# Second block of a two-block network on one core: router and first gather taken on the raw residual sum, expert weights queued one by one, dense weight units, expert tail in halves

## The chip, the cores and the metric

The kernel runs on one core of a Trainium2 chip, as one program. The metric is the device time of one execution in microseconds (us). The engines are TensorE (PE; PEld is its weight load), VectorE (DVE), ScalarE (ACT), GpSimd (POOL) and SyncE (SP), which only issues DMAs here.

## The reference

256 tokens of width 1024 go through two layers of a first block and one layer of a second block, all in float32. The change lies at the end of the second block:

```python
x = x + g_m * hybrid_mixer(h, ...)            # ends in  merged @ w_out
h = rms_norm_2(x, norm_ffn) * (1.0 + sc_f) + sh_f
x = x + g_f * moe_ffn(h, w_router, b_router, w1, b1, w2, b2)

# moe_ffn: 32 experts, each token takes the best 4
logits = h @ w_router + b_router
top_v, top_e = lax.top_k(logits, 4);  weights = softmax(top_v)
hcat = h[tok] @ w1[e] + b1[e]                 # w1[e]: 1024 x 2048
x_glu = minimum(hcat[:, ::2], 7);  x_lin = clip(hcat[:, 1::2], -7, 7)
y = (x_glu * sigmoid(1.702 * x_glu) * (x_lin + 1)) @ w2[e] + b2[e]   # w2[e]: 1024 x 1024
```

The weights of 32 experts are 384 MB in units of 1 MB, and every one is read once.

## The kernel before

Activations stay in SBUF as two tiles of 128 tokens (t = 0, 1). Dense products (`gemm`, `products`, L205 to L207) split every weight granule of 128 x 1024 floats in a high and a low part (`load_split`, `split_from`: ACT at L143, DVE or POOL at L147) and add three products. Granules are loaded by SP (L219) into four buffers `raw`; the parts have seven buffers each.

The second block's mixer ends with `merge`: for each of six pairs (branch, half of the columns) a gate of four granules and, one pair later, a branch product of two. `merge` calls `then` once, in the second round: `prepare` queues the vector `gf`, the router's weights `wr` and bias `br`, the experts' first biases `b1` (by way of two of the four `raw` buffers), and the first four expert units back to back (`unit`, L1482). The compiler's planner orders each engine's stream from costs and due times; only what is pinned (`pin`, `pe`) keeps the program's order. The new buffers lie where the sliding-window attention (swa) had its scratch.

Then comes the last projection `w_out_2` (eight granules), one granule for both token tiles and the other seven tile by tile, each closed by `done`: scale and add the residual (L1262, L1263), `rms_mod` (sums of squares at L861, a reciprocal root by Newton steps at L124 to L138, the modulation at L872 and L873 with the full rows `A` and `sh`, transposes at L233 with copies at L878). `route` computes the logits (L1310), the best four (L1312 to L1320), the places of the tokens (L1322 to L1326) and the counts (L1329); `moe_gather` builds a one-hot matrix (L1357) and gathers the tokens of two experts by matmuls (L1369, copied out at L1372).

The expert stage `moe` takes two experts at a time, 24 units a pair: `moe_up` (L1417) with eight pairs of units, the activation (L1425 to L1430), transposes (`moe_aT`, L1439), `moe_down` (L1456) with four pairs of units, scaling (L1461) and `combine` (L1526, L1527), which for the last pair also writes the output (L1529). The units go round a ring of 18 buffers (`mtile`): four early ones, five more on the right side, nine where the granules of the dense products had been (`low`), the last one (`mods`, tile `AS`) where `A` and `sh` had been. A unit is issued when its buffer is free. Row p * 8 + j of a weight goes to partition p, so a unit takes 8 KB from each partition's stretch of 64 KB (w1) or 32 KB (w2). For the last pair the second half of w2 comes as four units split by columns (L1487, pieces of 2 KB).

Of the kernel before, what the change touches and what calls it, by code (L numbers as in the profile page):

```python
# [71 lines left out]
class Kernel:  # L72
    def __init__(self, tc, a, out, dbg=None):
        self.tc, self.nc, self.a, self.out, self.dbg = tc, tc.nc, a, out, dbg
        self.n = 0
        self.nraw, self.nhl, self.next, self.xp = 4, 7, 4, None
        self.npj, self.ngt, self.glag = 4, 4, 1
        self.dtail = 8
        self.xg = 4
        self.sp, self.late = None, False  # L80
        self.pre, self.npre = [], 4
        self.start = False
# [31 lines left out]

    def small(self, n, tag="sm", dt=F32):
# [4 lines left out]
    def rsqrt(self, v, eps, n, scale=1.0):  # L120
# [6 lines left out]
        y = self.small(n, "ry")  # L127
# [81 lines left out]
    def load_split(self, nk, w, c0, width, xn=0, onpool=()):  # L209
# [5 lines left out]
        for i in range(ng):  # L215
# [3 lines left out]
            nc.sync.dma_start(raw.rearrange("p (k n) -> p k n", n=width), self.wsrc(w, i * kpg, m, c0, width))  # L219
# [452 lines left out]
    def merge(self, mp, lhs, w_in, g0, wb, yTs, order, nk, then=None):  # L672
# [178 lines left out]
    def rms_mod(self, t, h, A, sh, split=True):  # L851

# [9 lines left out]
        self.normed = nc.vector.tensor_tensor(ss[:, 2:3], ss[:, 0:1], ss[:, 1:2], op=OP.add)  # L862
        r = self.rsqrt(ss[:, 2:3], 1e-6, 1, 1.0 / D)
        xT = self.new_xT(t)
        def part(v, c):

            return v[:, c * 512:c * 512 + 512] if split else v.rearrange("t (p k) -> t k p", k=KD)[:, 4 * c:4 * c + 4]

        for c in range(2):
            s = slice(c * 512, c * 512 + 512)  # L870
            hv = h[:, s] if split else h[:, s].rearrange("t (k p) -> t k p", k=4)
            nc.vector.scalar_tensor_tensor(hv, part(x, c), r[:, 0:1], part(A, c), op0=OP.mult, op1=OP.mult)  # L872
            nc.vector.tensor_tensor(hv, hv, part(sh, c), op=OP.add)  # L873
            if split:
                self.to_T(h, t, xT[0], xT[1], 4 * c, 4)
            else:
                pt = self.trans4([h[:, k * P:k * P + P] for k in range(4 * c, 4 * c + 4)])
                nc.scalar.activation(xT[0].bitcast(F32)[:, 4 * c:4 * c + 4, :],  # L878
                                     pt.rearrange("p (k q) -> p k q", q=P), AF.Copy)
# [311 lines left out]
    def hybrid_in(self, ctx, gp, first):  # L1191
# [3 lines left out]
        with tc.tile_pool(name="mix2", bufs=1, reuse_waits="tile") as mp:  # L1195
            gm = self.st(gp, [P, D], "gm")
            self.mod_row(gm, 2)
            A, sh = self.mod_pair(self.mods, 3, a["norm_ffn_2"][0])
# [39 lines left out]
            def prepare():  # L1238
                bp = self.bp = ctx.enter_context(tc.tile_pool(name="blk2", bufs=1, side="right", reuse_waits="tile"))
                self.gf = bp.tile([P, D], F32, name="gf")  # L1240
                self.mod_row(self.gf, 5)
                self.route_prep(bp)
                self.sel = self.selector(0)
                units(self.npre)
                self.mi = 0
                for src in self.sources(0)[:self.npre]:
                    self.pre.append(self.unit(src))

            mg = self.merge(mp, lhs, w, 3328, a["w_branch_2"][0], yTs, (1, 0, 2), 4, prepare)
# [3 lines left out]
        units(self.na - self.npre)  # L1253
        hp = ctx.enter_context(tc.tile_pool(name="h2", bufs=1, side="right", reuse_waits="tile"))
        self.h2 = [hp.tile([P, D], F32, name=f"h{t}") for t in range(2)]
        with tc.tile_pool(name="y5", bufs=1, reuse_waits="tile") as fp:
            def done(t, banks):
                x = self.x[t]
                for h in range(2):
                    s = slice(h * 512, h * 512 + 512)  # L1260
                    y = self.st(fp, [P, 512], "y5", bufs=2)
                    nc.vector.scalar_tensor_tensor(y, banks[h], 0.5, gm[:, s], op0=OP.mult, op1=OP.mult)  # L1262
                    nc.vector.tensor_tensor(x[:, s], x[:, s], y, op=OP.add)  # L1263
                self.rms_mod(t, self.h2[t], A, sh, False)

            self.late = True
            self.gemm(self.lhs_x(mT), KD, a["w_out_2"][0], 0, D, done, tail=7)


    def route_prep(self, mp):  # L1270
        nc, a = self.nc, self.a
        wr = self.st(mp, [P, KD, NE], "wr")
        nc.gpsimd.dma_start(wr, a["w_router_2"][0].rearrange("(p k) n -> p k n", k=KD))
        br = self.st(mp, [P, NE], "br")
        nc.gpsimd.dma_start(br, arow(a["b_router_2"][0], NE))

        src = a["b1_2"][0].rearrange("e (j n) -> (e j) n", j=4)
        self.b1 = []
        for i in range(2):
            raw = self.st(self.wp, [P, 1024], "raw", bufs=self.nraw)[:, :512]  # L1280
            hl = self.st(mp, [P, 512], f"b1{i}", F32R)
            for h in range(2):
                nc.gpsimd.dma_start(raw[64 * h:64 * h + 64], src[64 * i:64 * i + 64])
            self.pin(nc.scalar.activation(hl, raw, AF.Copy))
# [3 lines left out]
        self.pin(nc.vector.tensor_tensor(self.pick, self.ident[:, :64], self.ident[:, 64:], op=OP.add))  # L1288
        tri = self.st(mp, [P, P], "tri")
        nc.vector.memset(tri, 1.0)  # L1290
# [3 lines left out]
        nc.vector.memset(one, 1.0)  # L1294
        self.rc = br, wr, tri, one

    def route(self, mp):

        nc, a = self.nc, self.a
        br, wr, tri, one = self.rc  # L1300
        self.W = self.st(mp, [P, 2, NE], "W")
        self.pos = self.st(mp, [P, 2, NE], "pos")
        mask = self.st(mp, [P, 2, NE], "mask")
        off = self.st(mp, [P, 2, NE], "off")
        cnt = self.st(mp, [P, NE], "cnt")
        for t in range(2):
            xT = self.xT[t][0].bitcast(F32)
            pl = self.ps("sc")[:, :NE]
            for k in range(KD):
                self.logits = nc.tensor.matmul(pl, xT[:, k, :], wr[:, k, :], start=k == 0, stop=k == KD - 1)  # L1310
            lg = self.st(mp, [P, NE], f"lg{t}")
            nc.vector.tensor_tensor(lg, pl, br, op=OP.add)  # L1312
            m8 = self.small(8, "m8")
            nc.vector.max(m8, lg)
            nm = self.small(1, "nm")
            nc.vector.tensor_scalar(nm, m8[:, 0:1], -1.0, None, op0=OP.mult)
            nc.vector.memset(m8[:, 4:8], 3.0e38)
            rep = self.st(mp, [P, NE], "rep")
            nc.vector.match_replace(rep, m8, lg, -3.0e38)
            nc.vector.tensor_tensor(mask[:, t], rep, lg, op=OP.not_equal)  # L1320
            pc = self.ps("sc")
            nc.tensor.matmul(pc[:, :NE], tri, mask[:, t], start=True, stop=t == 0)  # L1322
            if t:
                nc.tensor.matmul(pc[:, :NE], one, mask[:, 0], start=False, stop=True)
            nc.vector.tensor_scalar(off[:, t], mask[:, t], -BIG, BIG, op0=OP.mult, op1=OP.add)
            nc.vector.tensor_tensor(self.pos[:, t], off[:, t], pc[:, :NE], op=OP.add)  # L1326
            if t:
                for u in range(2):
                    nc.tensor.matmul(pc[:, NE:2 * NE], one, mask[:, u], start=u == 0, stop=u == 1)  # L1329
                nc.vector.tensor_copy(cnt, pc[:, NE:2 * NE])  # L1330
            ex = self.st(mp, [P, NE], f"ex{t}")
            nc.scalar.activation(ex, lg, AF.Exp, bias=nm)
# [3 lines left out]
            nc.vector.tensor_scalar(self.W[:, t], ex, sm, None, op0=OP.mult)  # L1336

# [5 lines left out]
        on = self.st(mp, [P, NE], "on")  # L1343
        nc.vector.memset(on, 1.0)
# [5 lines left out]
        self.Wh = self.st(mp, [P, 2, NE], "Wh")  # L1350
        nc.vector.tensor_scalar(self.Wh, self.W, 0.5, None, op0=OP.mult)

    def one_hot(self, mp, tag, pos):

        S = self.st(mp, [P, 2, 2, CAP], tag)
        for t in range(2):
            self.nc.vector.tensor_tensor(S[:, t], self.slot[:, None, :].to_broadcast([P, 2, CAP]),  # L1357
                                         pos[:, t, :, None].to_broadcast([P, 2, CAP]), op=OP.is_equal)
        return S

    def moe_gather(self, mp, pos):

        nc = self.nc
        S = self.one_hot(mp, "S", pos).rearrange("p t e s -> p t (e s)")
        xe = self.st(mp, [P, KD, P], "xe")
        pg = [self.ps("sc") for _ in range(2)]
        for t in range(2):
            for c in range(KD):
                self.pe(nc.tensor.matmul(pg[c // 4][:, c % 4 * P:c % 4 * P + P], self.h2[t][:, c * P:c * P + P], S[:, t],  # L1369
                                         start=t == 0 and c % 4 == 0, stop=t == 1 and c % 4 == 3))  # L1370
        for i in range(2):
# [391 lines left out]
```

## Time and profile before

| | us |
|---|---|
| median of 3 runs | 2553.19 (2549.77 to 2553.88) |
| the profiled execution | 2552.11 |
| its span, first to last instruction | 2550.5 |
| PE busy | 2385.5 (94%) |
| DVE, ACT, POOL busy | 1279.3, 817.6, 227.1 |
| mean granted clock of PE | 0.977 |
| moved by DMA | 707.49 MB |

Times in the rows count from the start of the span. Matmuls are pipelined, so a row's mean duration is more than the distance from one to the next. An arrow in brackets names what ended an engine's idle time.

### The profile page before, as it was taken

The page shows a single profiled execution, that of the slowest core. Times are in us where ns is not written, and L with a number is a line of the kernel's source. Part 1 is how long each engine was busy: PE and PEld are TensorE (multiplying, and loading weights), DVE is VectorE, ACT ScalarE, POOL GpSimd, SP SyncE. Part 2 cuts the span into 40 slices and gives each one's busy share as a digit, 9 for nine tenths or more (in the row PEclk, how much of TensorE's full clock was granted, in tenths as well). Part 3 has the DMA queues.
Part 4 walks back from the last instruction along what each step waited for, and adds up shares of the span by engine and source line. Part 5 has one row for each costly group of instructions (what it writes and reads, how often), then busy time and mean ns, then how long its engine had stood idle before and what let it go on. Part 6 is the DMA issues. An engine that isn't in the chain of part 4 may idle for free.

```text
span 2550.5 us, 29146 instructions
## 1 busy us (share of the span) xinstructions
PE 2385.5 (94%) x11076; PEld 1571.2 (62%) x11076; DVE 1279.3 (50%) x2126; ACT 817.6 (32%) x1161; POOL 227.1 (9%) x200
## 2 busy tenths in 40 slices
PE   7998999999799999989988988999889998999998
PEld 6887787778678878878867766433333333333332
DVE  6768757576666675675566756222222222222222
ACT  5443544444344454444435653100000010000000
POOL 4000211200200011230022101000000000000000
PEclk9999999999899999999999999999999999999999
DMA  8777465577667656665646367899999999999997
GB/s 267 243 235 232 145 185 181 181 224 226 195 197 234 193 151 185 189 197 175 182 153 214 109 215 265 364 421 421 421 421 421 421 421 421 421 421 421 421 421 285
DMA packets 203145, 707.49 MB, mean 277 GB/s; under 512 B 18090, under 2 KB 31610, under 8 KB 154360
## 3 DMA queue, kind: packets, MB, share of 16 engines
q1 hardware_dynamic: 195368, 684.02, 73.7%
q0 software_dynamic: 7632, 21.55, 2.8%
q8 instruction: 89, 1.46, 0.2%
q14 instruction: 56, 0.46, 0.1%
HBM read 704.39 MB, written 3.47 MB: 278 GB/s over the span
## 4 chain that ended last, share of the span: by engine, by line
PE 40%; DMA 36%; DVE 7%; issue 2%; ACT 2%; POOL 1%; SPq 0%; DVEq 0%; ACTq 0%; POOLq 0%
DMA mraw<-in_w_dram 28%; PE mm L206 10%; PE mm L207 10%; PE mm L205 10%; DMA AS<-in_w_dram 3%; PE mm L1417 3%; PE tp L233 2%; DVE wlo L147 2%; DMA raw<-in_w_in_dram 1%; PE sc L1456 1%; DMA araw<-in_w_ada_dram 1%; ACT whi L143 1%; POOL wlo L147 1%; PE sc L1369 1%; DVE x L274 0%
## 5 line engine op out<-in xcount | busy, mean ns | idle before, releaser
L147 DVE TENSOR_TENSOR wlo<-raw,whi 128x1024 fp32r<-128x1024 f32 (+1 forms) x459 | 568.1, 1244 | 304.4 <-ACT whi L143 302.0
L143 ACT ACTIVATE whi<-raw 128x1024 fp32r<-128x1024 f32 x486 | 509.8, 1055 | 546.9 <-PE mm L207 385.5
L205 PE MATMUL mm<-whi,xTh 128*128 128x512 f32 (+2 forms) x1552 | 598.4, 387 | 9.1 <-ACT whi L143 9.1
L206 PE MATMUL mm<-wlo,xTh 128*128 128x512 f32 (+2 forms) x1552 | 593.0, 383 | 13.0 <-POOL wlo L147 8.9
L207 PE MATMUL mm<-whi,xTl 128*128 128x512 f32 (+2 forms) x1552 | 592.6, 382 | 0.4 <-DVE xTl L147 0.4
L1417 PE MATMUL mm<-mraw,xe 128*64 128x512 f32 x1968 | 495.4, 615 | 49.3 <-DMA mraw<-in_w_dram 49.3
L1417 PEld LDWEIGHTS mm<-mraw,xe 128*64 128x64 f32 x1968 | 156.3, 141 | 367.2 <-issue 265.5
L206 PEld LDWEIGHTS mm<-wlo,xTh 128*128 128x128 f32 x1552 | 294.9, 190 | 73.9 <-POOL wlo L147 11.9
L205 PEld LDWEIGHTS mm<-whi,xTh 128*128 128x128 f32 x1552 | 294.8, 190 | 66.2 <-ACT whi L143 11.7
L207 PEld LDWEIGHTS mm<-whi,xTl 128*128 128x128 f32 x1552 | 294.8, 190 | 52.0 <-DVE xTl L147 1.0
L1426 ACT ACTIVATE mt<-mg 128x256 f32<-128x256 f32 x64 | 26.7, 417 | 812.4 <-DVE mg L1425 762.4
L1425 DVE TENSOR_SCALAR mg<-mm 128x256 f32<-128x256 f32 x64 | 27.2, 425 | 462.1 <-PE mm L1417 457.7
L1456 PE MATMUL sc<-mraw,xTl 128*64 128x512 f32 x936 | 223.4, 594 | 0.2 <-ACT xTl L1440 0.2
L1456 PEld LDWEIGHTS sc<-mraw,xTl 128*64 128x64 f32 x936 | 71.5, 137 | 140.2 <-issue 136.7
L207 PE MATMUL mm<-whi,hl 128*128 128x512 f32 x352 | 138.3, 393 | 0.0
L205 PE MATMUL mm<-whi,hh 128*128 128x512 f32 x352 | 138.1, 392 | 0.0
L206 PE MATMUL mm<-wlo,hh 128*128 128x512 f32 x352 | 138.0, 392 | 0.0
L1461 DVE TENSOR_TENSOR xTh<-sc,gf 128x512 f32<-128x512 f32 x32 | 22.1, 692 | 215.7 <-PE sc L1456 215.7
L822 DVE SCALAR_TENSOR_TENSOR acc<-araw,cond,acc 128x512 f32<-128x512 f32 x96 | 71.8, 748 | 52.5 <-DMA araw<-in_w_ada_dram 51.9
L147 POOL TENSOR_TENSOR wlo<-raw,whi 128x1024 fp32r<-128x1024 f32 x27 | 69.0, 2569 | 281.3 <-ACT whi L143 277.7
L694 POOL TENSOR_TENSOR pj<-pj,gt 128x512 f32<-128x512 f32 x32 | 59.1, 1861 | 193.2 <-DVE gt L693 192.6
L206 PEld LDWEIGHTS mm<-wlo,hh 128*128 128x128 f32 x352 | 66.7, 189 | 13.7
(416 smaller groups left out, 2144.4 us busy)
## 6 DMA issues: line engine op xcount, KB each, us to landing
mraw<-in_w_dram SPq DMA_DIRECT2D x362, 1024.0 KB, 19.8
raw<-in_ffn_up_dram SPq DMA_DIRECT2D x176, 512.0 KB, 4.5
raw<-in_w_in_dram SPq DMA_DIRECT2D x142, 512.0 KB, 4.4
raw<-in_ffn_down_dram SPq DMA_DIRECT2D x88, 512.0 KB, 4.3
araw<-in_w_ada_dram SPq DMA_DIRECT2D x96, 256.0 KB, 4.1
AS<-in_w_dram SPq DMA_DIRECT2D x21, 1024.0 KB, 19.8
raw<-in_w_branch_dram SPq DMA_DIRECT2D x28, 512.0 KB, 3.7
raw<-in_w_out_dram SPq DMA_DIRECT2D x24, 512.0 KB, 4.4
```

The costliest lines, as they stand in the source:

```text
L143: ins = self.nc.scalar.activation(hi, src, AF.Copy)
L147: ins = (self.nc.gpsimd if pool else self.nc.vector).tensor_tensor(lo, src, hi, op=OP.subtract)
L205: nc.tensor.matmul(banks[b], xh, hi[:, s], start=kc == 0, stop=False)
L206: nc.tensor.matmul(banks[b], xh, lo[:, s], start=False, stop=False)
L207: nc.tensor.matmul(banks[b], xl, hi[:, s], start=False, stop=kc == nk - 1)
L233: self.nc.tensor.transpose(pt[:s.shape[-1], i * P:i * P + s.shape[0]], s, self.ident)
L694: nc.gpsimd.tensor_tensor(m, m, th, op=OP.add)
L822: nc.vector.scalar_tensor_tensor(acc, raw, self.cond[:, k:k + 1], acc, op0=OP.mult, op1=OP.add)
L1417: self.pe(nc.tensor.matmul(ph[nb][e * 64:e * 64 + 64], xe[:, k, e * 64:e * 64 + 64], units[e][k][:, nb * 512:nb * 512 + 512], start=False, ...
L1425: nc.vector.tensor_scalar(g, pv[:, :, 0], 7.0, None, op0=OP.min)
L1426: nc.scalar.activation(th, g, AF.Tanh, scale=0.851)
L1456: self.pe(nc.tensor.matmul(py[c][e * 64:e * 64 + 64], aT[:, k * P + e * 64:k * P + e * 64 + 64], w, start=k == 0, stop=k == 7))
```

## The change

- `merge` calls `step` twice a round. Step 0 loads biases and `gf` and queues the first unit (in `mods`, now free, since `A` and `sh` are replaced by two columns per partition, `mod_cols`); steps 6 to 9 queue one unit each; from step 0 on the granules' loads and the early units keep the program's order on SP (`steady`). `b1` is loaded into buffers of its own.
- The last projection takes four granules for both tiles, then the other four bank by bank (`part`), and the last bank's four in two halves; PE, DVE and ACT keep the written order (`ordered`). `residual` leaves x + g * y in `h2`; squares go on beside it. Router and gather use this sum: the scale is folded in `wr`, the shift in `br`, and 1/rms is multiplied in at the best-four step (`choose`) and into the one-hot matrix. Scale and shift are applied where the gathered tokens are copied out (`gather_end`, eight operations shared by DVE and ACT). The gather of tile 0 is done ahead of the logits of tile 1. Counts and softmax (`route_rest`) come behind the first `moe_up`.
- A unit is now a dense stretch of 1 MB of w1 or w2. Column block nb of the hidden layer then needs w2 unit nb alone: `moe_body` turns and multiplies block by block. The last pair's last two units come as four DMAs of half a unit, one per half of the columns, and each half is scaled, combined and written by itself.

```diff
-        self.pre, self.npre = [], 4
+        self.pre, self.npre = [], 5
...
+            if self.steady:
+                self.pin(ins)
...
-            if i == 1 and then:
-                then()
+            if then:
+                then(2 * i)
             if i >= lag:
                 branch(*todo[i - lag], first=todo[i - lag][0] == order[0])
+            if then:
+                then(2 * i + 1)
...
+            def step(i):
+                if i == 0:
+                    self.bp = ctx.enter_context(tc.tile_pool(name="blk2", bufs=1, side="right", reuse_waits="tile"))
+                    self.ring.append(self.mods)
+                    units(self.npre - 1)
+                    self.mi = 0
+                    self.route_load(self.bp, late)
+                    self.steady = True
+                if i == 0 or 6 <= i < 5 + self.npre:
+                    self.pre.append(self.unit(self.sources(0)[len(self.pre)], True))
+                if i == 8:
+                    self.route_prep(self.bp, late)
...
+    def out_and_route(self, lhs, grans, gm):
...
+        for g in grans[:4]:
+            for t in range(2):
+                self.products(lhs, KD, D, banks[t], t, [g])
+        rest = grans[4:]
...
+        self.part(lhs, 0, banks[0][0], 0, rest)
+        self.residual(0, 0, banks[0][0], gm)
+        self.part(lhs, 0, banks[0][1], 1, rest)
+        self.residual(0, 1, banks[0][1], gm)
+        self.part(lhs, 1, banks[1][0], 0, rest)
+        self.residual(1, 0, banks[1][0], gm)
+        self.turn(0, 0)
+        self.turn(0, 1)
+        self.part(lhs, 1, banks[1][1], 1, rest[:2])
+        self.logits(0, 0)
+        self.logits(0, 1)
+        self.choose(0)
+        self.part(lhs, 1, banks[1][1], 1, rest[2:])
+        self.place(0)
+        self.turn(1, 0)
+        self.residual(1, 1, banks[1][1], gm)
+        self.gather_begin()
+        self.logits(1, 0)
+        self.turn(1, 1)
+        self.logits(1, 1)
+        self.ph0 = self.moe_bias(self.sel, self.b1[0], 3)
+        self.choose(1)
+        self.place(1)
+        self.ph0 += self.moe_bias(self.sel, self.b1[0], 1, 3)
...
+    def residual(self, t, h, bank, gm):
+        nc.vector.scalar_tensor_tensor(y, bank, 0.5, gm[:, s], op0=OP.mult, op1=OP.mult)
+        nc.vector.tensor_tensor(self.h2[t][:, s], self.x[t][:, s], y, op=OP.add)
+        nc.scalar.activation(y, self.h2[t][:, s], AF.Square, accum_out=ss[:, h:h + 1])
+        if h == 0:
+            nc.vector.tensor_scalar(ss[:, 2:3], ss[:, 0:1], 1.0 / D, 1e-6, op0=OP.mult, op1=OP.add)
+        else:
+            self.rsqrt(ss[:, 1:2], ss[:, 2:3], 1, 1.0 / D, out=self.rn[:, t:t + 1])
...
+    def moe_body(self, mp, ph, act, aT, ys, units, end=None):
+        py = [self.ps("sc") for _ in range(2)]
         for nb in range(4):
+            self.moe_act(mp, act, ph[nb], nb)
+        self.moe_aT(act, aT, 0)
+        for nb in range(1, 4):
+            self.moe_aT(act, aT, nb)
+            self.moe_down(py, aT, units, nb - 1)
+        for c in range(2):
+            if end or c == 0:
+                self.moe_down(py, aT, units, 3, (c,) if end else (0, 1), bool(end))
+            self.moe_scale(ys, py, c)
+            if end:
+                end(c)
...
+        up = [of(W1, d).rearrange("(k p) n -> p k n", p=P)[:, k] for k in range(KD) for d in range(2)]
+        return up + [of(W2, d).rearrange("(j p r) n -> p j (r n)", p=P, r=2)[:, j] for j in range(4) for d in range(2)]
```

## Rows read from the trace of the kernel before

**Rows 1.** The page: GB/s moved in 40 equal slices of the span.
```profile
GB/s 267 243 235 232 145 185 181 181 224 226 195 197 234 193 151 185 189 197 175 182 153 214 109 215 265 364 421 421 421 421 421 421 421 421 421 421 421 421 421 285
```

**Rows 2.** Windows: us, busy PE PEld DVE ACT POOL, PE clock, DMA share, GB/s.
```profile
1515.00:1525.00 10.00, 3.02 (x8) 1.65 (x7) 2.30 (x2) 2.93 (x3) 0.00 (x0) 0.71 0.97 377
...
1605.00:1607.00 2.00, 2.00 (x11) 2.00 (x11) 0.32 (x3) 0.00 (x0) 0.00 (x0) 0.50 0.38 156
1607.00:1613.00 6.00, 6.00 (x35) 3.48 (x35) 0.49 (x2) 1.19 (x2) 0.00 (x0) 0.92 0.00 1
1613.00:1615.00 2.00, 2.00 (x12) 0.68 (x10) 0.00 (x0) 0.00 (x0) 0.00 (x0) 1.00 0.53 127
1615.00:1625.00 10.00, 10.00 (x50) 3.32 (x48) 0.00 (x0) 0.00 (x0) 0.00 (x0) 1.00 1.00 421
...
2525.00:2528.00 3.00, 2.75 (x16) 1.38 (x18) 0.00 (x0) 1.09 (x2) 0.00 (x0) 1.00 0.68 260
2528.00:2531.50 3.50, 3.50 (x20) 1.21 (x18) 0.00 (x0) 0.00 (x0) 0.00 (x0) 1.00 0.39 147
2531.50:2541.00 9.50, 9.50 (x42) 3.12 (x40) 1.95 (x3) 0.00 (x0) 0.00 (x0) 1.00 0.00 0
```

**Rows 3.** Timeline of SP around the merge and the start of the experts: issues.
```profile
1503.97 3.06 SPq L1482 DMA_DIRECT2D mraw<-in_w_dram  x4
...
1557.87 31.29 SPq L1482 DMA_DIRECT2D mraw<-in_w_dram  x13
...
1612.94 24.93 SPq L1482 DMA_DIRECT2D mraw<-in_w_dram  x16
```

**Rows 4.** The chain of waits in the merge: start, us, what.
```profile
1505.27 1.29 DVE b L1285 x2
...
1507.14 14.26 DMA raw<-in_w_in_dram
```

**Rows 5.** Timeline of PE in the merge: start, us, instruction, idle before it.
```profile
1522.58 1.22 PE L205 MATMUL mm<-whi,xTh 128*128 128x512 f32 x2 [6.94 <-ACT whi L143]
```

**Rows 6.** Timeline of PE, DVE and ACT in the last projection and behind it.
```profile
1573.73 0.69 DVE L1262 SCALAR_TENSOR_TENSOR y<-mm,gm 128x512 f32<-128x512 f32 x1 [3.34 <-PE mm L207]
...
1578.05 2.28 DVE L872 SCALAR_TENSOR_TENSOR h<-x,ry,AS 128x512 f32<-128x512 f32 x2
...
1581.45 0.63 PE L233 MATMUL tp<-ident,h 128*128 128x128 f32 x4 [1.71 <-DVE h L873]
...
1586.38 0.69 DVE L1262 SCALAR_TENSOR_TENSOR y<-mm,gm 128x512 f32<-128x512 f32 x1 [2.69 <-PE mm L207]
...
1596.78 0.60 ACT L878 ACTIVATE xTh<-tp 128x512 f32<-128x512 f32 x1 [0.42 <-PE tp L233]
...
1602.44 1.06 PE L1329 MATMUL sc<-mask,one 128*128 128x32 f32 x4 [0.28 <-DVE pos L1326]
```

**Rows 7.** The chain that ended last, pieces from the modulation to the end.
```profile
1591.41 2.09 DVE h L872 x2
...
1598.16 1.72 PE sc L1310 x16
1603.50 5.83 PE sc L1369 x32
1609.33 27.62 PE mm L1417 x128
1636.95 3.78 PE sc L1369 x32
...
2540.39 1.92 PE sc L1456 x8
```

**Rows 8.** Timeline of DVE at the end of the last pair: the second half's scaling.
```profile
2542.33 0.69 DVE L1461 TENSOR_TENSOR xTh<-sc,gf 128x512 f32<-128x512 f32 x1 [1.21 <-PE sc L1456]
```

**Rows 9.** DMA issues by line: count, KB each, median us to landing.
```profile
raw<-in_w_in_dram SPq DMA_DIRECT2D x142, 512.0 KB, 4.4
...
raw<-in_w_out_dram SPq DMA_DIRECT2D x24, 512.0 KB, 4.4
```

More of the change, by code (lines that the diff above doesn't have):

```diff
@@ L113, in pin, with ordered @@
         self.tc.keep_in_program_order(ins)
+    @contextmanager
+    def ordered(self):
+        cur = self.nc.cur_bb
+        traced = cur.bb.instructions
+        last = traced[-1]
+        yield
+        assert self.nc.cur_bb is cur
+        start = next(k for k in reversed(range(len(traced))) if traced[k] is last) + 1
+        chain = mybir.DependencyInfo(mybir.DependencyClass.NoSync, mybir.DependencyReason.DATA)
+        for engine in (mybir.EngineType.PE, mybir.EngineType.DVE, mybir.EngineType.Activation):
+            prev = next((i for i in reversed(traced[:start]) if i.engine == engine), None)
+            for i in traced[start:]:
+                if i.engine == engine:
+                    if prev is not None:
+                        self.tc.add_manual_dep(i, prev.name, chain, reason="ordered")
+                    prev = i
     def small(self, n, tag="sm", dt=F32):
@@ L1236, in units @@
                         tc.tile_pool(name=self.nm("moewa"), bufs=1, side="right", reuse_waits="tile")))
[L1238 to L1249, printed above, removed]
+            def step(i):
[10 more added lines that the diff above has]
+                    self.route_prep(self.bp, late)
+            with tc.tile_pool(name="late", bufs=1, reuse_waits="tile") as late:
+                mg = self.merge(mp, lhs, w, 3328, a["w_branch_2"][0], yTs, (1, 0, 2), 4, step)
             mT = [self.new_xT(t) for t in range(2)]
@@ new lines, in place @@
+    def place(self, t):
+        nc = self.nc
+        tri, one = self.rc[1:3]
+        off = self.st(self.bp, [P, NE], "off")
+        nc.vector.tensor_scalar(off, self.mask[:, t], -BIG, BIG, op0=OP.mult, op1=OP.add)
+        pc = self.pr[:, (2 + t) * NE:(3 + t) * NE]
+        if t:
+            nc.tensor.matmul(pc, one, self.mask[:, 0], start=True, stop=False)
+        nc.tensor.matmul(pc, tri, self.mask[:, t], start=t == 0, stop=True)
+        nc.vector.tensor_tensor(self.pos[:, t], off, pc, op=OP.add)
@@ L1305, in route, with gather_begin, route_rest @@
+    def gather_begin(self):
+        self.pg0 = [self.ps("sc") for _ in range(2)]
+        self.S0 = self.st(self.bp, [P, 2, 2, CAP], "S0")
+        self.one_hot(self.S0, 0, self.pos[:, :, 0:2], self.rn)
+        self.gather_tile(self.pg0, self.S0, 0)
+    def route_rest(self, mp):
+        nc = self.nc
+        br, tri, one, on = self.rc
+        mask = self.mask
         cnt = self.st(mp, [P, NE], "cnt")
+        pc = self.ps("tp")[:, :NE]
+        for u in range(2):
+            nc.tensor.matmul(pc, one, mask[:, u], start=u == 0, stop=u == 1)
+        nc.vector.tensor_copy(cnt, pc)
@@ L1326, in route @@
[L1326 to L1330, printed above, removed]
             ex = self.st(mp, [P, NE], f"ex{t}")
-            nc.scalar.activation(ex, lg, AF.Exp, bias=nm)
+            nc.scalar.activation(ex, self.lg[t], AF.Exp, bias=self.nm8[t])
             sm = self.small(1, "sw")
@@ L1380, in moe_back @@
+        for t in range(2):
+            self.one_hot(S, t, pos, w)
         pw = self.ps("tp")
@@ new lines, in moe_aT, with moe_down @@
+    def moe_aT(self, act, aT, nb):
+        pt = self.ps("tp")
+        for r in range(2):
+            self.pe(self.nc.tensor.transpose(pt[:, r * P:r * P + P], act[:, nb, r], self.ident))
+        self.nc.scalar.activation(aT[:, nb * 256:nb * 256 + 256], pt[:, :256], AF.Copy)
+    def moe_down(self, py, aT, units, j, cs=(0, 1), last=False):
+        for r in range(2):
+            for c in cs:
+                o = c * D + r * 512 if last else r * D + c * 512
+                for e in range(2):
+                    k = (2 * j + r) * P + e * 64
+                    self.pe(self.nc.tensor.matmul(py[c][e * 64:e * 64 + 64], aT[:, k:k + 64], units[e][j][:, o:o + 512],
+                                                  start=j == 0 and r == 0, stop=j == 3 and r == 1))
```

384 lines of the change are left out of this document (200 added, 184 removed).

## Prediction

> **What bounds the kernel now.** I read the page's slices first, then the windows, the timelines around the merge, and the chain that ended last. The slices show two regimes [rows 1]: up to slice 25 some 110 to 270 GB/s, then 421 in every slice to the last but one. So the expert stage runs at the pace of its loads, and work saved inside it is worth nothing. Its time is set by when the unbroken stream starts, how many bytes are then left, and what follows the last byte.
>
> The windows show the start [rows 2]. At 1605.8 (share 0.38 of the 2 us from 1605) the loads stop, stay at 1 GB/s from 1607 to 1613, and begin again near 1613.9 (share 0.53 of the 2 us from 1613). SP tells why: four units are issued at 1503.97, then 13 from 1557.87 and one more, and the next only at 1612.94 [rows 3]. That is the ring of 18: all full, and none is free until the first `moe_up` has used its first pair of units. That `moe_up` starts at 1609.33 [rows 7]. From its start to flowing data are 4.6 us, and from 1613.9 on 366 units are left whatever happens before.
>
> The windows show the end too: the last loads are thin (share 0.68, then 0.39) and over by 2531.5 [rows 2]; the span closes at 2550.5, so 19.0 us follow the last byte.
>
> Two places ahead of the start are open. In the merge PE stands for 6.94 us [rows 5], waiting for a granule whose load took 14.26 us [rows 4], since four units had gone out just before it [rows 3]; it could not go earlier, because the biases `b1` held two of the four `raw` buffers until their split at 1505.27 [rows 4]. And between the last projection's last bank (DVE takes it at 1586.38 [rows 6]) and `moe_up` lie 22.95 us of serial steps.
>
> **The change, part by part.**
>
> *Units in the merge.* Removed: the burst of four, and the hold on `raw`. A unit takes 1.0486 MB / 421 GB/s = 2.49 us, so a granule behind one waits about that long, not 14.26. Upper bound of the gain: the stall of 6.94 and, as an estimate from a clock of 0.71 in that window [rows 2], 1.5 us of slow matmuls behind it: 8.4. Lower bound 0: the buffers of units 2 to 5 lie over the attention's scratch, which before let none of them go earlier than 1503.97 [rows 3]. They are now pinned ahead of branch granules. If SP stands at the first of them until then, the granules behind it come a unit (2.49) and a landing (4.4 [rows 9]) later, some 7 us in all, and the old stall is back at another place. I take 5.0, above the middle, because the first unit uses a buffer that is free early and the granules ahead of the block have four `raw` buffers. POOL's loads for step 0 are the old ones bar the router's weights; behind them stand the merge's additions, as before. `mod_cols` swaps three full-row loads and a multiplication on POOL for small column loads much earlier; costed at nothing, covered by the attention between, and worth a few us of waiting if a chain behind them on POOL is late.
>
> *Last projection.* Its matmuls stay the same. PE's wait for the modulation, 1.71 [rows 6], goes; the logits of tile 0, 1.72 [rows 7], now stand ahead of its last part. The transposes of tile 0 were there before. Net 0.
>
> *From the last bank to `moe_up`.* DVE, PE and ACT keep the written order, so I follow it from the moment DVE takes the last bank. Residual, squares and reciprocal root: tile 0 did them from 1573.73 to 1578.05 [rows 6], 4.3. The places of tile 0 and its two one-hot operations, on DVE around it: 0.8 (estimate). Gather of tile 0, half of 32 matmul entries: 2.9 by the 5.83 of the first gather, 1.9 by the 3.78 of a later one [rows 7]. Then, behind it on PE, half the logits (0.86), four transposes (0.63), a copy (0.60) with its handing over (0.3), the other half (0.86): 3.3 [rows 6, 7]. Best four, places and one-hot of tile 1: before they took 1598.16 + 1.72 = 1599.88 to 1603.50, of which 1.06 was the counts [rows 6, 7], which leave: 2.6. The second half of the gather 2.9 or 1.9; the first copy out 0.6; five more handings over 1.0. Together 18.4 with slow gathers, 16.4 with fast ones. The modulation (2.09 and as much again), the biases' matmuls and the counts are gone from the path or beside it.
>
> Which gather? At 1605 to 1607, after waits on DVE, the granted clock was 0.50 [rows 2], the level of 1.2 GHz, while the later one, between dense matmuls, ran at full clock. In the new order PE waits over 4 us for DVE ahead of the first half, so I take 18.4; gain 22.95 - 18.4 = 4.5, between 0 (every handing over as slow as now) and 6.5.
> The Trainium skill ("TensorE: Matmul & The Clock Gate", Part 1: The HAM clock gate) says the clock falls back to half once the engine has been idle and rises only after it has been busy again; by that both halves are slow and the path is 18.4, against 16.4 by the later row. The row at 0.50 agrees.
>
> What is late next: nothing in front of the stream. `moe_up` starts 5.0 + 4.5 earlier and the ring has to be full by then. Seven buffers lie where the projection's granules were; 7 x 2.49 = 17.4 us, less than 18.4 + 4.6, so the ring still waits for `moe_up`, and the stream's start moves by the whole 9.5.
>
> *The stage itself.* Block-wise `moe_body`, eight copies in place of two, and the earlier `combine` are costed at nothing: the stream at 421 GB/s covers them. Were PE the bound, they would count. Dense units: rows of w_out are loaded dense, pieces of w_in are not, and both land in 4.4 us [rows 9]; nothing, bounds in the rivals.
>
> *The end.* 366 units at 2.49 are 911.6 us; the loads took 1613.9 to 2531.5 = 917.6, 6.0 more, of which 1.0 + 2.1 are the thin windows. Half as many units come in 2 KB pieces now: gain 2.4, between 0 and 4.5. After the last byte: the first half's products wait for nothing but their own half unit, which lands 2.5 earlier. Then PE combines it, about 1.9, runs the second half's four products, 1.92 [rows 7], hands over (0.3), and the close follows that today begins with the scaling at 2542.33 [rows 8] and takes 8.2: 12.3 against 19.0, gain 6.7 (3, if the clock is low and PE falls behind; 9, if the first combine hides).
>
> Sum: 5.0 + 0 + 4.5 + 2.4 + 6.7 = 18.6. The profiled execution took 2552.1, so 2533.5; the median of the runs lies 1.1 above it: **2534.5**.
>
> **The rivals.**
>
> *SP stands at the pinned unit.* As priced above, the merge gives 0: 2539.5. For it: 1503.97, and an SP that takes its list in order. Against: one buffer's wait need not be the latest of the four. If the chain gives nothing either, 2544.
>
> *The dense layout slows the stream (slower).* Sixteen engines then read side by side in one stretch of 1 MB. The gain of 18.6 is gone if the 917.6 us grow by 2.0%, at 413 GB/s; at 405 it is 36 us more, less 18.6: 2570. For it: no saturated dense stream is in the trace. Against: equal landings [rows 9], and the rate did not move between w1 and w2, whose strides differ by two [rows 1].
>
> *The layout speeds it up.* If strides cost something now, 1% more rate is 9 us: at 430 GB/s 19 us less, 2515. Against it: 421 in every slice looks like a limit of the engines.
> The Trainium skill ("DMA: Bandwidth & Descriptors", Latency and other measured facts) reports that row pitches at large powers of two cut the rate and that dense tiles restore it; the equal landings here speak against it at these strides.
>
> *Nothing arrives.* PE falls behind at half clock at the end, and the start's gain is lost in later waits: within 5 us of now.
>
> **How the numbers follow.** Forecast 0.62, its own range 2525 to 2544 (merge 0 to 8.4, chain 0 to 6.5, end 3 to 13, seldom all at one side). SP blocked 0.22. Slower by layout 0.06, faster by layout 0.05, nothing 0.05. The range for 8 in 10 takes in the second and the upper edge of the fast layout: 2515 to 2546. What can be told from no change is 0.2%, 5 us: faster 0.62 + 0.22 + 0.05 = 0.89, same 0.05, slower 0.06.
>
> **What would show it.** Right: no stall of PE near 1515; the idle window of the loads shrinks and ends near 1604; 421 GB/s behind it; 12 us from the last load to the end. Wrong: SP's early unit followed by PE waiting for a branch granule; `moe_up` more than 21 us behind the last bank; windows of the stage off 421 by over 1%; PE still multiplying well after the last byte.

## The result: 1.4% slower, and the profile after

| | before | after |
|---|---|---|
| median of 4 runs each, us | 2551.61 (2549.77 to 2553.88) | 2587.45 (2585.15 to 2590.28) |
| the profiled execution, us | 2552.11 | 2586.45 |
| its span, us | 2550.5 | 2584.9 |

The ratio is 1.0141 (1.0123 to 1.0158): slower, outside the range of 2515 to 2546 and on the side that had a chance of 0.06. One execution behind the numbers below, of the kernel without granule pins, took 12399 us; it counts in no ratio.

The page of the changed kernel shows where to look: its GB/s in 40 slices.

```profile
GB/s 266 239 243 226 145 195 179 179 228 246 170 214 224 197 141 189 183 190 182 193 172 151 25 261 189 301 420 420 421 420 421 420 421 421 421 421 421 421 421 328
```

From the 27th slice to the last but one it reads as in [rows 1], 420 to 421: the stage runs at its old rate. New is the slice of 25 GB/s, the 23rd, between 1422 and 1486 us. The windows (columns as in [rows 2]) of the kernel before over the attention and the merge:

```profile
1440.00:1500.00 60.00, 56.57 (x285) 44.73 (x284) 44.49 (x84) 34.85 (x69) 5.39 (x5) 1.00 0.42 125
1500.00:1560.00 60.00, 51.90 (x232) 41.71 (x232) 37.54 (x39) 28.46 (x34) 13.52 (x12) 0.94 0.80 276
```

and those of the changed kernel, there and at the last projection, in the stage and at the end:

```profile
1440.00:1500.00 60.00, 33.16 (x120) 23.73 (x121) 29.57 (x71) 19.62 (x55) 5.95 (x14) 0.53 0.12 36
1500.00:1560.00 60.00, 60.00 (x260) 49.13 (x259) 35.33 (x33) 30.06 (x32) 3.53 (x2) 0.98 0.89 302
...
1618.00:1622.00 4.00, 1.94 (x9) 1.37 (x8) 2.03 (x7) 1.69 (x4) 0.00 (x0) 0.92 0.56 233
1622.00:1626.00 4.00, 4.00 (x18) 3.81 (x18) 0.86 (x6) 0.00 (x0) 0.00 (x0) 0.50 0.01 4
...
1700.00:2560.00 860.00, 811.52 (x3614) 300.70 (x3612) 222.12 (x510) 70.05 (x190) 0.00 (x0) 0.98 1.01 421
2564.00:2566.00 2.00, 2.00 (x10) 0.53 (x5) 0.00 (x0) 0.38 (x1) 0.00 (x0) 1.00 0.75 296
...
2568.00:2570.00 2.00, 2.00 (x12) 0.65 (x10) 0.00 (x0) 0.00 (x0) 0.00 (x0) 1.00 0.60 226
2570.00:2572.00 2.00, 1.80 (x8) 0.34 (x4) 0.16 (x1) 0.00 (x0) 0.00 (x0) 1.00 0.22 83
2572.00:2574.00 2.00, 1.41 (x4) 0.68 (x4) 0.78 (x2) 0.00 (x0) 0.00 (x0) 1.00 0.00 0
```

Before, PE worked 56.57 of the 60 us from 1440, with 285 matmuls: the attention's, and between them products of the merge. After, 33.16 us with 120 matmuls at half clock (0.53): all but a few of them the attention's. The products come behind it, in a stretch without a gap (60.00 of 60) but longer than the one it replaces. The timeline of the changed kernel (SP, then ACT and DVE) says who let the merge wait:

```profile
1404.10 10.37 SPq L237 DMA_DIRECT2D raw<-in_w_in_dram  x4
1499.23 1.50 SPq L237 DMA_DIRECT2D raw<-in_w_branch_dram  x2
...
1496.40 0.60 ACT L161 ACTIVATE yT2h<-tp 128x512 fp32r<-128x512 f32 x1 [0.26 <-PE tp L253]
1496.89 3.88 ACT L161 ACTIVATE whi<-raw 128x1024 fp32r<-128x1024 f32 x4
...
1497.97 4.63 DVE L165 TENSOR_TENSOR wlo<-raw,whi 128x1024 fp32r<-128x1024 f32 x4 [0.25 <-ACT whi L161]
```

SP loads the second gate's four granules by 1414.5 and then nothing for 85 us: the four `raw` buffers are full. They come free when ACT and DVE split them, and in both engines' streams these splits now stand right behind the attention's last split (`yT2h`), at 1496.9. ACT was busy 19.62 of the 60 us: it had the time, but not the order.

Three moments divide the rest: DVE takes the last bank of the last projection; SP issues the first unit into a used buffer of the ring (from there the stream is unbroken); the span ends.

| us | last bank | stream starts | span ends | bank to start | start to end |
|---|---|---|---|---|---|
| before | 1586.38 | 1612.94 | 2550.5 | 26.6 | 937.6 |
| after | 1628.12 | 1652.28 | 2584.9 | 24.2 | 932.6 |
| change | +41.7 | +39.3 | +34.4 | -2.4 | -5.0 |

So the path behind the last bank and the end brought 7.4 us, and 41.7 were lost ahead of the last bank. PE's last four transposes of the merged tiles (1561.81 before, 1591.39 after) divide these 41.7: 29.6 arose in the merge, up to these transposes, and 12.2 between them and the last bank, in the last projection (24.6 before, 36.7 after).

### The profile page after: what moved, and what is told of

It is laid out like the page before. It is cut to its first block, busy times and chain, and to the rows that moved or that the text cites. A ratio compares the mean times of both kernels' runs of the same rounds, so it can differ in the third digit from the quotient of the medians.

```text
span 2584.9 us, 29398 instructions
## 1 busy us (share of the span) xinstructions
PE 2418.6 (94%) x11078; PEld 1584.9 (61%) x11078; DVE 1308.0 (51%) x2231; ACT 830.6 (32%) x1227; POOL 225.7 (9%) x203
## 4 chain that ended last, share of the span: by engine, by line
PE 54%; DMA 21%; DVE 8%; ACT 3%; issue 2%; POOL 1%; SPq 0%; ACTq 0%; DVEq 0%; POOLq 0%
DMA mraw<-in_w_dram 18%; PE mm L224 11%; PE mm L225 11%; PE mm L223 11%; PE mm L1574 8%; PE sc L1605 6%; PE tp L253 2%; PE tp L1680 1%; DVE wlo L165 1%; PE sc L1503 1%; ACT whi L161 1%; DMA araw<-in_w_ada_dram 1%; POOL wlo L165 1%; DMA raw<-in_w_ple_gate_dram 1%; DVE x L294 0%
## 5 line engine op out<-in xcount | busy, mean ns | idle before, releaser
L1574 PE MATMUL mm<-mraw,xe 128*64 128x512 f32 x1920 | 483.0, 608 | 36.2 <-DMA mraw<-in_w_dram 36.2
L1585 ACT ACTIVATE mt<-mg 128x256 f32<-128x256 f32 x64 | 26.6, 416 | 692.0 <-DVE mg L1584 692.0
L1605 PE MATMUL sc<-mraw,xTl 128*64 128x512 f32 x976 | 231.9, 598 | 7.5 <-ACT xe L1514 7.5
L1681 DVE TENSOR_TENSOR x<-x,tp 128x512 f32<-128x512 f32 x68 | 46.7, 687 | 131.6 <-PE tp L1680 131.6
```

The source lines that it names most:

```text
L1574: self.pe(nc.tensor.matmul(ph[nb][e * 64:e * 64 + 64], xe[:, k, e * 64:e * 64 + 64], units[e][k][:, nb * 512:nb * 512 + 512], start=False, ...
L1605: self.pe(self.nc.tensor.matmul(py[c][e * 64:e * 64 + 64], aT[:, k:k + 64], units[e][j][:, o:o + 512], start=j == 0 and r == 0, stop=j == ...
L1681: nc.vector.tensor_tensor(self.x[t][:, s], self.x[t][:, s], po, op=OP.add)
```

## The experiments

Theory A: the pins on SP's loads changed the order of ACT, DVE and PE, which the planner makes, and put the merge behind the attention. Rival B: SP stands at a pinned unit. Rival C: the written order of projection and routing costs it. Rival D: the first unit itself is in the way.

**The first unit free.**

```diff
-self.pre.append(self.unit(self.sources(0)[len(self.pre)], True))
+self.pre.append(self.unit(self.sources(0)[len(self.pre)], i > 0))
```

> The only edit: the first expert unit is no longer pinned to its place on SP's queue behind the first gate's granules (units 2 to 5 and all granules stay pinned). Theory A: the 1.4% were lost because the pinned order, from the first gate's last granule over the first unit to the second gate's granules, put all splits and products of the merge from the second gate on behind the attention; undone, about 190 of the 432 products that PE ran behind the attention go back beside it, 190 x 0.226 us = 43 us, of which the attention takes some 7 back: about 2550 us, between 2535 and 2558, and PE multiplies over 50 of the 60 us from 1440 to 1500. Rival B: SP stands at units 2 to 5, which wait for the attention's scratch: those are unchanged, so the time stays within 5 us of 2587. Rival C: the written order of the last projection and the routing costs it: also within 5 us of 2587.

Measured: 2550.97 us, ratio to before 0.9992 (0.9979 to 1.0006). The 36.5 us are back, from one pin, with projection, routing, layout and tail unchanged: C falls as the main cause. The path and the end gain as well, 6.2 and 5.1 us on the kernel before by the profile; but the last bank comes 9.8 later (1596.17), 0.9 of it up to the merge's last transposes and 8.9 in the last projection. The chain of waits in the merge:

```profile
1502.23 0.23 POOL tri L1374
1502.45 0.12 SPq L1636
...
1502.62 7.73 DMA raw<-in_w_branch_dram
...
1510.37 1.06 ACT whi L161
...
1511.48 1.22 PE mm L223 x2
```

And SP's longest wait from 1460 to 1510 (line, what it waited for, us in total, times, longest):

```profile
SPq L1636 <- DVE s L1191: 34.7, 1, 34.7
```

SP, which had issued nothing since 1466.8, stands 34.7 us at a pinned unit (L1636), whose buffer lies over the attention's scratch `s`, and is let go at 1502.45; the branch granule behind it lands 7.73 later, and PE stands 8.69. B holds too, as a second loss that the first had hidden: it is the stall of [rows 5] at another place.

**No pins on granules** (units still pinned).

```diff
-            if self.steady:
-                self.pin(ins)
```

> The only edit: the merge's granules are not pinned to the program's order on SP's queue any more; all five early units are. Theory A (the order chain lost the overlap): as the first experiment or a little better, 2530 to 2555 us. Rival B (SP stands at the pinned units): a granule can now be queued ahead of a unit that waits, so this too would gain, but the first experiment would not. Rival C (last projection and routing): stays within 5 us of 2587.

Measured: 2539.86 us, 0.9942 (0.9921 to 0.9962). Its windows:

```profile
1440.00:1500.00 60.00, 57.81 (x287) 46.50 (x286) 47.20 (x82) 38.50 (x67) 5.39 (x5) 1.00 0.57 176
1500.00:1560.00 60.00, 56.81 (x265) 46.96 (x264) 39.46 (x48) 27.70 (x40) 16.97 (x19) 0.97 0.86 307
```

The overlap is there (287 matmuls) and the stall is not. A and B both foretold a gain here; with the first experiment they are two losses of one cause, the pinned order.

**Pins, but no early unit.**

```diff
-if i == 0 or 6 <= i < 5 + self.npre:
+if 6 <= i < 6 + self.npre:
```

> All pins stay, but no unit is queued at the merge's first step: the five early units follow from the seventh step on. Theory A in its narrow form (the chain of pins holds the second gate back, with or without a unit in it): stays at 2580 to 2592 us, with PE idle beside the attention as in the changed kernel. Rival D (the unit itself, its buffer or its transfer ahead of the second gate's granules, holds them back): gains as the first experiment, 2535 to 2558.

Measured: 2583.70 us, 1.0134 (1.0112 to 1.0156). SP's timeline:

```profile
1401.99 10.38 SPq L237 DMA_DIRECT2D raw<-in_w_in_dram  x4
1497.14 1.50 SPq L237 DMA_DIRECT2D raw<-in_w_branch_dram  x2
...
1516.95 0.42 SPq L1636 DMA_DIRECT2D AS<-in_w_dram  x1
```

No unit is queued before 1516.95, and the gap of the loads is the same: D falls, and so does B for the main loss. What holds the merge is the chain of pins from the first gate's granules to the second's.

The first experiment kept all pins on granules too, and yet had its overlap back. SP's timeline there shows what differs:

```profile
1327.85 0.34 SPq L1636 DMA_DIRECT2D AS<-in_w_dram  x1
```

In the program the unpinned unit stands between the two gates' granules; it went out far ahead of both. The two runs fit together if a pin ties a load to the one in front of it in the program, so that the free unit was a gap in the chain, while here the gates are tied directly. That is inferred from the two runs and not tried by itself.

**The pins in the kernel before.**

```diff
-            nc.sync.dma_start(raw...)
+            ins = nc.sync.dma_start(raw...)
+            if self.steady:              # set in merge, behind the first gate
+                self.pin(ins)
```

> The kernel before, with one thing added: the loads of the merge's granules behind the first gate's (and of the last projection) are pinned to the program's order on SP's queue, as the change does; no unit is moved, nothing else of the change is in. Theory A: these pins alone push the splits and products from the second gate on behind the attention: 2552 + 33 = 2585 us, between 2575 and 2592, with PE busy for some 33 of the 60 us from 1440 to 1500. Rival H: the pins do that only together with the changed early loads: within 6 us of 2552.

Measured: 2597.91 us, 1.0175 (1.0154 to 1.0195), more than expected, and by another way than Theory A's:

```profile
1397.92 19.33 SPq L219 DMA_DIRECT2D raw<-in_w_in_dram  x6
1501.39 2.16 SPq L1485 DMA_DIRECT2D mraw<-in_w_dram  x4
1503.65 1.06 SPq L219 DMA_DIRECT2D raw<-in_w_branch_dram  x2
...
1519.22 1.22 PE L205 MATMUL mm<-whi,yT1h 128*128 128x512 f32 x2 [17.97 <-ACT whi L143]
```

The pins put the first branch's granules behind the burst of four units, which wait for the scratch until 1501.39. That is B at full price: 84 us without a load and a stall of 17.97. The pins alone are enough for a loss of this size, but not for Theory A's: PE still worked 42.71 of the 60 us from 1440, with 169 matmuls, well over the changed kernel's 33.16. How pins cost time depends on what stands next to them.

**Logits behind the last part** (on the first experiment's kernel): tile 0's `logits` and `choose` follow the whole last `part`.

> The first experiment's kernel, with the logits of tile 0 and the choice of its experts moved behind the last part of the last projection. In the changed kernel PE stood 2.06 us for their transposes' copy in front of that part, spent 3.62 us on them at half clock, and ran the part's six matmuls at half clock (3.1 in place of 1.4 us). Theory E: some 7 us on the path ahead of the last bank, of which the choice and the places of tile 0, now behind the last residual on DVE, take about 2.5 back: 4 to 5 us less than the first experiment. Rival F: whatever stands ahead of the last bank only trades places with what follows it: within 2 us of the first experiment.

Measured: 2551.26 us, 1.0001 (0.9990 to 1.0013), so F. From the merge's last transposes to the last bank it took 29.2 us against 33.5 in the first experiment, 4.3 less; from there to the stream's start 24.4 against 20.4, 4.0 more.

**The last units whole** (on the kernel without granule pins): no `halves`, both banks closed behind the last two whole units.

> The second experiment's kernel (no pins on granules), with the last two units of the last pair loaded whole and dense in place of four halves in 2 KB pieces, and both banks closed behind them. Theory I (the halves' pieces cost about what the shorter close gains): the last byte comes some 3 us earlier, since the loads no longer run at a share of 0.6 to 0.75 at their end; the close grows from 13.8 by four more products (1.9) and the first combine that was hidden (about 2.2): 1 us more, 2538 to 2544 us in all. Rival J (the halving is worth the 6.7 us of the forecast): 2545 to 2548.

Measured: 2541.17 us, 0.9958 (0.9942 to 0.9973), 1.3 over the kernel with halves (3.1 over its repeat below), within the intervals. The sum is Theory I's, its first half is not. Windows of the last loads:

```profile
2516.00:2518.00 2.00, 2.00 (x11) 0.80 (x7) 0.00 (x0) 0.00 (x0) 0.00 (x0) 1.00 0.77 311
2518.00:2520.00 2.00, 2.00 (x8) 0.53 (x8) 0.00 (x0) 0.38 (x1) 0.00 (x0) 1.00 0.65 266
2520.00:2522.00 2.00, 2.00 (x12) 0.78 (x10) 0.00 (x0) 0.00 (x0) 0.00 (x0) 1.00 0.57 238
2522.00:2524.00 2.00, 0.75 (x4) 0.00 (x0) 0.00 (x0) 0.00 (x0) 0.00 (x0) 1.00 0.22 90
```

Whole dense units of 8 KB pieces thin out just as the halves do (0.75 to 0.22 above). The last load's last packet ends at 2523.5 here and at 2524.6 with halves, 918.7 and 918.8 us behind the stream's start (1604.8 and 1605.9); only the close differs, 15.7 against 13.7. So the halving is worth 2 us, not 6.7, and the pieces of 2 KB don't cause the thin end.

**Tile 0's gather first** (on the kernel without granule pins).

```diff
-        self.part(lhs, 1, banks[1][1], 1, rest[2:])
+        self.part(lhs, 1, banks[1][1], 1, rest[2:3])
         self.place(0)
+        self.part(lhs, 1, banks[1][1], 1, rest[3:])
         self.turn(1, 0)
-        self.residual(1, 1, banks[1][1], gm)
         self.gather_begin()
+        self.residual(1, 1, banks[1][1], gm)
```

> The second experiment's kernel, with the places and the gather of tile 0 written ahead of the last residual (the places between the two halves of the last part's products), so that DVE makes tile 0's one-hot before the last bank's residual. Theory K: in the changed order PE stands 4.2 to 4.6 us for the one-hot behind the residual and gathers tile 0 only then; ahead of it, that gather lies beside the residual, and the path from the last bank to the stream's start loses 3 to 5.5 us: 2534.5 to 2537 us. Rival L: PE only waits for the residual's transposes at another place, and DVE starts the residual later by the one-hots (1.0): within 1.5 us of 2540.

Measured: 2528.60 us, 0.9910 (0.9888 to 0.9931). PE's timeline without the edit, and with it:

```profile
1577.70 2.85 PE L1427 MATMUL mm<-wr,xTh 128*128 128x32 f32 x16 [2.07 <-ACT xTh L1419]
1588.63 3.76 PE L1501 MATMUL sc<-S,h 128*128 128x128 f32 x16 [4.18 <-DVE S L1497]
...
1598.23 3.76 PE L1501 MATMUL sc<-S,h 128*128 128x128 f32 x16
```

```profile
1570.53 2.68 PE L1428 MATMUL mm<-wr,xTh 128*128 128x32 f32 x16 [2.07 <-ACT xTh L1420]
...
1577.21 2.53 PE L1502 MATMUL sc<-S,h 128*128 128x128 f32 x16
...
1585.34 3.62 PE L1502 MATMUL sc<-S,h 128*128 128x128 f32 x16
```

The wait of 4.18 for the one-hot `S` is gone and the first gather runs beside the residual. From last bank to stream it now takes 16.0 us against 22.2. K holds in its mechanism, with a little more than it foretold. The median fell by 11.3 us, more than the path's 6.2; the rest lies ahead of the last bank, where profiles of one kernel differ by 5 us, and within the intervals.

With the shorter path another limit comes into play, as the loads between the last bank and the stream show (windows of the kernel without granule pins, then of both orders, the next experiment):

```profile
1602.00:1604.00 2.00, 2.00 (x10) 0.69 (x12) 0.82 (x2) 1.21 (x5) 0.00 (x0) 0.88 0.00 0
```

```profile
1596.00:1598.00 2.00, 2.00 (x12) 0.62 (x10) 0.00 (x0) 0.00 (x0) 0.00 (x0) 1.00 0.86 287
```

Without granule pins all loads stop for 6.4 us before the stream starts (4.5 in the repeat's profile). With both orders the packets show no gap over 0.3 us from 1579.7 on. The units that wait for the projection's last buffers load for 16.6 us in both profiles without granule pins; a path of 16.2 is now as long as these loads, and a shorter one could hardly start the stream earlier.

**Both orders**: also `turn(0, 0)` and `turn(0, 1)` ahead of `residual(1, 0)`, so that ACT's copies don't stand behind the squares.

> As the kernel with the gather first, and the transposes of tile 0 written ahead of the residual of the first bank of tile 1, so that ACT copies them before that residual's squares. Theory M: ACT's copies stood behind the squares; PE's 2.07 us in front of tile 0's logits goes, and with it some of the half clock on the logits (2.85 against 1.7) and on the products behind: 2 to 4 us less than with the gather first alone, 2531 to 2535 us. Rival F, as for the logits moved behind the last part: it trades places with what follows the last bank, within 1 us of the kernel with the gather first.

Measured: 2527.94 us, 0.9900 (0.9881 to 0.9919). The wait of 2.07 went: from its first bank to its last the projection took 11.4 us, against 15.4 with the gather first alone. The time did not move measurably; the intervals are wider than what M and F differ by, so the medians decide between neither. Once more, beside the kernel without granule pins:

> The second experiment's kernel once more, beside the three that follow, since its median stood on five runs: 2535 to 2541 us. Its distance to the kernel with both reorderings is what the path from the last bank to the stream's start is worth: 6.8 us by the two profiles (23.0 against 16.2) and some 3 more ahead of the last bank, 7 to 11 us.

> Tile 0's gather ahead of the last residual and its transposes ahead of the residual before, once more: 2525 to 2530 us, a ratio to the kernel before of 0.988 to 0.992.

Measured: 2538.06 us, 0.9938 (0.9924 to 0.9951), and 2526.20 us, 0.9894 (0.9879 to 0.9909). Both repeat; their distance, 11.9 us, is a little over the 7 to 11 foretold. Both orders without granule pins make the kernel that beats before (by 1.1%) and after.

**Products to hold the clock.** 27 products whose result is not read, in PE's two waits:

> The second experiment's kernel with 27 products more, whose result nobody reads: 9 in front of tile 0's logits and 18 in front of its gather, where PE stood 2.07 and 4.18 us; everything else as there. Theory N (half clock behind idle PE is a term of its own): the granted clock stays at 1.0 up to the gather, so the logits (2.85), the last six products and tile 0's gather (3.76) run at the full clock's times (1.7, 1.4, 1.9): 3 to 5 us less than the second experiment, 2532 to 2536 us. Rival O (DVE sets the path, and PE's clock only moves its waits): within 1.5 us of the second experiment.

Measured: 2539.80 us, 0.9953 (0.9937 to 0.9968). It tests less than it should: the products made a wait of their own. PE's and ACT's timeline:

```profile
1577.86 4.38 PE L1318 MATMUL sc<-whi,xTh 128*128 128x512 f32 x18
...
1582.28 0.60 ACT L1427 ACTIVATE xTh<-tp 128x512 f32<-128x512 f32 x1 [7.88 <-PE sc L1318]
```

ACT's copy of transposes that PE had finished in front of the 18 products was let go only behind them, and the squares for the last residual stood behind it. The kernel's text offers a reason: the copy writes tile 1's `hT`, which `turn` takes by `new_xT` from a pool of one buffer, and the 18 products read what lay in that buffer before (`lhs(0, kc, 1)`). By that the copy had to let them finish; products that read another tile were not tried in this place. The logits did run faster, 1.97 in place of 2.85. Four such products in the kernel with both orders, in a wait of 0.69:

> The kernel with both reorderings, with 4 products more, not read, in PE's wait of 0.69 us for the last copy ahead of tile 1's second half of logits; there the granted clock falls at 1585.5 and tile 1's gather takes 3.76. Theory N: the clock holds, that gather takes 1.9 and the first expert products run at full clock: 1 to 3 us less than the kernel with both reorderings. Rival O: within 1 us of it.

Measured: 2526.27 us, 0.9890 (0.9874 to 0.9905). PE's timeline:

```profile
1583.76 1.18 PE L1317 MATMUL tp<-b 128*128 128x512 f32 x4
...
1588.32 2.05 PE L1508 MATMUL sc<-S,h 128*128 128x128 f32 x16
```

The gather of tile 1 took 2.05 against 3.76, and from last bank to stream it took 13.4 us against 16.2. Whether the four products did that is open: without any, this gather took 3.76 in one profile of the kernel without granule pins and 2.05 in the other. The median shows none of the 2.7 us. They lie within the intervals, and the profile shows that most of them could not count: the loads ran without a pause here, as they had without the products,

```profile
1596.00:1598.00 2.00, 2.00 (x12) 0.65 (x10) 0.00 (x0) 0.00 (x0) 0.00 (x0) 1.00 0.99 406
```

and from the stream's start to the end it took 934.7 us against 932.7, so 2.0 of the 2.7 came back as loads that were still to be done. So neither experiment could tell what the clock is worth on this path.

## Why the prediction was wrong

**The merge: the step that failed.** "Lower bound 0", with 5.0 taken, and as the worst case "SP stands at the first of them". The pins were priced on SP's own queue, as if the rest of the streams stayed. The text before the prediction says that the planner orders every stream and that a pin fixes program order; so the pins also changed the order of ACT, DVE and PE, and the work at stake was the whole overlap with the attention: 29.6 us later at the merge's last transposes, 41.7 at the last bank. The row that would have shown the size is the busy PE of 1440 to 1500, which was not read; the prediction began its rows at 1503. A bound below zero belonged there. Why the planner ranks the second gate's splits behind the attention once the loads are chained stays open: the trace shows the order, not its reason.

**SP at the pinned unit.** The rival was right in its mechanism and price (some 7 us foretold; a landing of 7.73 and a stall of 8.69 in the first experiment), but not as what decided: the changed kernel never reached it. Without granule pins the last bank came 2.7 and 8.1 us before that of the kernel before, in two profiles of one kernel, and the forecast of 5.0 lies between. That is luck: up to the merge's last transposes these profiles are 9.5 and 14.7 us ahead, more than the upper bound of 8.4, and the last projection then takes 6.7 and 6.6 back.

**Last projection, 0: a second step that failed.** From the merge's last transposes to the last bank it took 24.6 us before, 36.7 after, and 31.3 and 31.2 without granule pins. In the changed kernel the products start late, since ACT splits the first four granules only behind its copies for these transposes (before, it split the first at 1543.36), and they start at half clock (0.50 from 1594 to 1598); later PE waits for tile 0's copies and runs the logits at half clock too:

```profile
1561.81 0.60 PE L233 MATMUL tp<-ident,pj 128*128 128x128 f32 x4
```

```profile
1591.39 0.63 PE L253 MATMUL tp<-ident,pj 128*128 128x128 f32 x4 [0.46 <-DVE xTl L165]
1592.55 3.89 ACT L161 ACTIVATE whi<-raw 128x1024 fp32r<-128x1024 f32 x4
1593.65 0.49 PE L223 MATMUL mm<-whi,xTh 128*128 128x512 f32 x1 [1.63 <-ACT whi L161]
...
1621.37 3.62 PE L1429 MATMUL mm<-wr,xTh 128*128 128x32 f32 x16 [2.06 <-ACT xTh L1421]
...
1633.07 3.78 PE L1503 MATMUL sc<-S,h 128*128 128x128 f32 x16 [4.48 <-DVE S L1499]
...
1644.91 3.76 PE L1503 MATMUL sc<-S,h 128*128 128x128 f32 x16
```

(The first line is the kernel before's, the others the changed kernel's.) The logits cost 3.62, not the 1.72 taken. Moving them behind the last bank made the projection 4.3 us shorter and the path behind it 4.0 longer, so that part can be booked in either place. In place of 0 the term measured a loss of 6.7 without granule pins and of 12.2 with them.

**Last bank to stream, gain 4.5.** Measured 2.4 after, and 4.4 and 6.0 without granule pins (22.2 and 20.5 against 26.6): right in mechanism, and inside 0 to 6.5. The sum of 18.4 up to `moe_up` met 18.2 in the first profile without granule pins, where both gathers ran slow as taken; in the changed kernel it was 20.5, with both gathers slow (3.78 and 3.76) and tile 1's logits too (1.75 and 1.91 where 0.86 was taken). What the step did not see is that tile 0's gather need not be on the path at all; written ahead of the residual it saves 4 to 6 us more, until the loads themselves fill the path.

The Trainium skill ("TensorE: Matmul & The Clock Gate", Part 1: The HAM clock gate) says that how many matmuls run at the half clock varies between runs of one kernel. The traces agree: tile 1's gather took 3.76 in one profile of the kernel without granule pins and 2.05 in the other.

**The end, gain 2.4 + 6.7.** Measured 5.0 together. Start to last byte (2571.1 after, 2531.2 before) is 918.8 against 918.3: the 2.4 was put on the pieces of 2 KB, and the whole units show that they cost nothing. From last byte to end it is 13.8 against 19.3, 5.5 of the 6.7, in the bounds of 3 to 9; the halving itself is worth 2.0 of it; what the other 3.5 came from was not tried by itself.

**The layout.** 421 GB/s in both kernels: neither rival on it came true.
The Trainium skill ("DMA: Bandwidth & Descriptors", Latency and other measured facts) reports a loss of rate at row pitches of large powers of two, in figures from 512 KiB up; no run here shows one at 32 and 64 KB.

**The sum.** Foretold: 5.0 + 0 + 4.5 + 9.1 = 18.6 (which gives a median of 2534.6, not 2534.5). The kernel without granule pins has 2.7 + 4.4 + 5.1 = 12.2 by its profile, which is its gain in span. The forecast described roughly that kernel, and its 2.7 is 9.46 gained in a merge foretold at 5.0 less 6.75 lost in a projection foretold at 0; the changed kernel has the pins.

## What to carry to other kernels

Where a planner orders the streams, a pin on one queue can change all of them, as it did here: look for the overlap that the loads feed (PE's busy share beside the stage in front) and price its loss as the lower bound. Where two losses have one cause, undoing one shows the other, so take away the whole cause and each part of it. On a chain of small steps, first ask which of them need the last bank at all: two calls moved ahead of the residual took 11 us off the median, of which the profiles show 4 to 6 on the path itself. Look at the loads before shortening such a path further: once they run without a pause, a shorter path hardly counts. Time the stage in front of a changed path too: the last projection, which took in part of its work, became 6.7 us longer, more than the 4.4 and 6.0 gained behind it.

## What the runs showed that was not expected

The end of an unbroken stream thins out over some 7 us (shares 0.77, 0.65, 0.57, 0.22 with pieces of 8 KB, 0.75, 0.67, 0.60, 0.22 with 2 KB); why stays open.

Products put into a wait of PE made ACT wait 4 us, although nobody reads their result: by the kernel's text, what they read lay in the buffer that ACT's next copy writes.

Two profiles of one kernel reached the last bank 5.4 us apart (1583.68 and 1578.32), yet their spans from stream start to end were 932.4 and 932.7: what differs between these two lies ahead of the stream.
